# Expert products of 16 more tokens of block 2 from gathered U rows, in a decoder block on one Trainium2 core

## The chip, the cores and the metric

One core of one Trainium2 chip runs the kernel as one program. The metric is device time in microseconds (us) of one execution, the median of several runs. TensorE multiplies matrices, VectorE and ScalarE work on elements, GpSimd (POOL) does a few element operations here and writes the descriptors of indirect DMAs, SyncE (SP) issues most loads. All five run their own queues in order and meet through semaphores.

## The reference, cut to what matters

One layer of a decoder: a mixer (state-space heads beside latent attention) with a normalisation, and then PEER, an expert layer, with another. The change touches PEER alone:

```python
def peer(x, w_query, sub_keys, u_table, v_table):      # T = 128 tokens a block, 4 blocks
    ...
    def block(xb):
        q = (xb @ w_query).reshape(T, 8, 2, 128)
        s = jnp.einsum('thkd,hknd->thkn', q, sub_keys)
        sv, si = lax.top_k(s, 16)
        ...                                            # 16 of 16384 experts for each of 8 heads
        gate = jax.nn.softmax(top_s, axis=-1)
        u = jnp.take(u_table, expert_idx, axis=0)
        act = gelu(jnp.einsum('td,thkd->thk', xb, u))
        v = jnp.take(v_table, expert_idx, axis=0)
        return jnp.einsum('thk,thkd->td', gate * act, v)
```

Each of the 512 tokens has 128 experts; the tables hold 16384 rows of 1024 numbers each.

## The kernel before

Tokens are dealt with in two ways. **Dense:** U (16384 x 1024, loaded once as 128 chunks of 128 experts) is multiplied with all tokens of blocks 0 and 1 and the first half of block 2, so that a chunk's activations lie in `acts` as 128 experts x 320 tokens (`NU` = 320, `u_half`, L1402). Products are made of three float32r products each of rounded parts and remainders (`mm3`, L84): high part (`h`, ScalarE, L126) and low part (`l`, VectorE or GpSimd, L136) of each chunk of 128 x 1024. A chunk is 8 x 3 matmuls, done in two halves of 12. **Gathered:** for the other tokens the experts' rows themselves are fetched by indirect DMA, 128 rows of 4 KB at a time, one a partition, and VectorE multiplies each with its token's x and sums (a dot, L1140). In this way 64 tokens of block 2 (`UG` = 64) have their activations from 64 fetches; the halves of the partitions hold two experts of a token. Block 3 is done wholly by gathering, U rows and then V rows, behind.

V is multiplied densely for 384 tokens (`NT`): a matrix of gates (expert x token, mostly zeros) is built for them, G, multiplied with the activations and with V chunk by chunk (`v_chunk`, L1680; 18 matmuls of 512 columns). For the 64 gathered tokens the activations are multiplied into the gates already when these are made, so that their 64 columns of activations aren't read (L1638).

The order is emitted by hand: one Python program writes all queues. Around the change it is:

- `stage1` and `stage2` (L1031, L1113): top-16 searches and decoding of expert numbers, on VectorE. When block 2 is decoded, `ug_index` (L1119) writes the index list and issues the first four fetches (`UROWS` = 4 buffers `urow`).
- `build_g` (L1205): 48 groups `n` of 8 tokens. For each, VectorE makes `oj` (L1228) and `g` (L1234) one group ahead (`hot`), ScalarE scales half of `g` in the groups of `LOWA`, TensorE multiplies them (16 small matmuls, L1270 and L1271) into `pw`, ScalarE moves the result to `stg`, which is stored to DRAM. Each fourth group also multiplies finished gates into the activations at hand (L1294).
- In the same loop two dots of `ug_dots` (L1137) follow each group, and after every dot the fetch of the row four further (`ug_fetch`, L1131), into the buffer just read. When all are done, the activations of the second partition half go through DRAM to the first (L1144), and `ug_head` (L1150) multiplies them with the gates at groups 35 to 38.
- `drive` (L1465) puts U halves between: `tm[0]` sums the planned time of TensorE (3.6 a chunk, 1.2 a group), `tm[1]` that of VectorE (1.2 a dot, 1.2 a low part, and so on), and as long as the first isn't ahead, it emits another half, until chunk 76 (`AHEAD`), or 85 once `ug_dots` is done. In groups below 32 there are two stops for this: after `hot`, and after the dots. A half that begins a chunk also emits the high part of the chunk three further and the low part of the chunk two further (`Stream`, L93).
- Activations of chunks 0 to 49 stay in SBUF, those of 50 to 87 are spilled to DRAM (L1417).
- Behind it the V stage: U chunks from 85 on alternate with V chunks, beside them block 3's 256 dots (`gather`, L1525).

PSUM has eight banks: two `px`, four `pw`, two `pu` in this part.

## Time and profile before

| | |
|---|---|
| median of 3 runs | 1539.13 us (1536.28 to 1540.73) |
| the profiled execution | 1538.01 us; its span 1536.2 us |
| TensorE busy | 1519.5 us, 99% of the span |
| VectorE busy | 1353.5 us, 88% |
| ScalarE busy | 755.0 us, 49% |
| GpSimd busy | 646.0 us, 42% |
| TensorE's granted clock | 0.998 of full speed over the span |
| bytes moved by DMA | 418.58 MB |

Busy time counts an instruction from its start to its end, and matmuls overlap: one of 320 columns is busy 0.31 us but the next starts 0.147 us later. So TensorE's pace is read from starts. L with a number is a line of the kernel. In lists of groups, `out<-in` are the program's names, then come partitions x elements, the count, the busy time and the mean of one, and behind the bar the time for which the engine sat idle just before them, with what ended it. PE is TensorE, DVE VectorE, ACT ScalarE.

### The profile page before, as it was taken

The page shows a single profiled execution, that of the slowest core. Times are in us where ns is not written, and L with a number is a line of the kernel's source. Part 1 is how long each engine was busy: PE and PEld are TensorE (multiplying, and loading weights), DVE is VectorE, ACT ScalarE, POOL GpSimd, SP SyncE. Part 2 cuts the span into 40 slices and gives each one's busy share as a digit, 9 for nine tenths or more (in the row PEclk, how much of TensorE's full clock was granted, in tenths as well). Part 3 has the DMA queues.
Part 4 walks back from the last instruction along what each step waited for, and adds up shares of the span by engine and source line. Part 5 has one row for each costly group of instructions (what it writes and reads, how often), then busy time and mean ns, then how long its engine had stood idle before and what let it go on. Part 6 is the DMA issues. An engine that isn't in the chain of part 4 may idle for free.

```text
span 1536.2 us, 24606 instructions
## 1 busy us (share of the span) xinstructions
PE 1519.5 (99%) x8664; PEld 1338.5 (87%) x8664; DVE 1353.5 (88%) x2641; ACT 755.0 (49%) x1415; POOL 646.0 (42%) x472
## 2 busy tenths in 40 slices
PE   9999999999999999999999999999999999999997
PEld 7787888888888999999999988999999988888886
DVE  8979768746799999999999588999999999999997
ACT  5564477742433444666667544444444434444442
POOL 0000032420244522445430476666666667767610
PEclk9999999999999999999999999999999999999999
DMA  7243122475423566999998999999999999999983
GB/s 261 95 149 102 57 71 60 111 250 162 155 76 90 146 214 213 338 347 365 383 323 289 367 401 387 384 380 395 401 398 400 392 393 380 390 378 390 373 300 135
DMA packets 154028, 418.58 MB, mean 272 GB/s; under 512 B 15296, under 2 KB 57040, under 8 KB 153648
## 3 DMA queue, kind: packets, MB, share of 16 engines
q1 hardware_dynamic: 96000, 210.83, 39.7%
q0 software_dynamic: 52496, 187.74, 32.7%
q10 hardware_dynamic: 5408, 18.43, 3.0%
q8 instruction: 68, 1.11, 0.3%
q14 instruction: 56, 0.46, 0.1%
HBM read 384.08 MB, written 30.70 MB: 270 GB/s over the span
## 4 chain that ended last, share of the span: by engine, by line
PE 91%; DVE 5%; ACT 2%; DMA 1%; issue 1%; ACTq 0%; DVEq 0%
PE va L1675 11%; PE va L1674 11%; PE va L1678 11%; PE pu L85 10%; PE pu L87 10%; PE pu L86 10%; PE pw L85 3%; PE pw L86 3%; PE pw L87 3%; PE pa L86 3%; PE pa L87 3%; PE pa L85 3%; PE pw L1270 1%; PE pw L1271 1%; PE pb L534 1%; PE px L1008 1%
## 5 line engine op out<-in xcount | busy, mean ns | idle before, releaser
L126 ACT ACTIVATE wih<-wir 128x1024 fp32r<-128x1024 f32 (+2 forms) x269 | 277.0, 1031 | 128.8 <-PE va L1678 71.7
L136 DVE TENSOR_TENSOR wil<-wir,wih 128x1024 fp32r<-128x1024 f32 (+1 forms) x232 | 280.5, 1210 | 54.5 <-ACT wih L126 39.3
L87 PE MATMUL pu<-XT,wil 128*128 128x320 f32 x1000 | 309.3, 309 | 0.6 <-DVE wil L136 0.6
L1675 PE MATMUL va<-wil,Ph 128*128 128x512 f32 x726 | 283.1, 390 | 0.0
L1541 POOL DMA_INDIRECT row<-v,ix x128 | 217.6, 1700 | 99.6 <-DVE ac L1562 78.3
L1674 PE MATMUL va<-wih,Ph 128*128 128x512 f32 x606 | 236.2, 390 | 0.0
L1541 POOL DMA_INDIRECT row<-u,ix x128 | 180.2, 1408 | 131.9 <-DVE row L1556 69.5
L85 PE MATMUL pu<-XT,wih 128*128 128x320 f32 x664 | 208.4, 314 | 0.8 <-ACT aout L1416 0.8
L86 PE MATMUL pu<-XT,wih 128*128 128x320 f32 x664 | 205.2, 309 | 0.0
L87 PEld LDWEIGHTS pu<-XT,wil 128*128 128x128 f32 x1000 | 187.8, 188 | 0.9 <-DVE wil L136 0.9
L1678 PE MATMUL va<-wih,Pl 128*128 128x512 f32 x606 | 186.8, 389 | 0.0
L1562 DVE SCALAR_TENSOR_TENSOR ac<-row,hd,ac 128x1024 f32<-128x1024 f32 x128 | 164.2, 1283 | 4.6 <-DMA row<-v,ix 3.1
L1556 DVE SCALAR_TENSOR_TENSOR row<-row,XT 128x1024 f32<-128x1024 f32 x128 | 153.9, 1222 | 12.1 <-DMA row<-u,ix 11.4
L1675 PEld LDWEIGHTS va<-wil,Ph 128*128 128x128 f32 x726 | 136.4, 188 | 26.9
L1134 POOL DMA_INDIRECT urow<-u,uix x64 | 100.4, 1569 | 136.7 <-DVE urow L1140 120.8
L1657 ACT ACTIVATE Ph<-P 128x384 fp32r<-128x384 f32 x121 | 63.0, 520 | 155.9 <-DVE P L1634 141.1
L136 POOL TENSOR_TENSOR wil<-wir,wih 128x1024 fp32r<-128x1024 f32 (+3 forms) x37 | 77.8, 2110 | 145.1 <-ACT wih L126 120.9
L1678 PEld LDWEIGHTS va<-wih,Pl 128*128 128x128 f32 x606 | 113.7, 188 | 23.9
L1674 PEld LDWEIGHTS va<-wih,Ph 128*128 128x128 f32 x606 | 113.7, 188 | 22.7 <-ACT Ph L1657 0.3
L85 PEld LDWEIGHTS pu<-XT,wih 128*128 128x128 f32 x664 | 124.7, 188 | 2.3 <-ACT aout L1416 1.4
L86 PEld LDWEIGHTS pu<-XT,wih 128*128 128x128 f32 x664 | 124.8, 188 | 0.8
L85 PE MATMUL pu<-XT,wihx 128*128 128x320 f32 x336 | 104.9, 312 | 0.9 <-ACT aout L1416 0.9
(511 smaller groups left out, 3332.6 us busy)
## 6 DMA issues: line engine op xcount, KB each, us to landing
wir<-v SPq DMA_DIRECT2D x106, 512.0 KB, 7.1
wir<-ut SPq DMA_DIRECT2D x86, 512.0 KB, 6.1
wirx<-ut SPq DMA_DIRECT2D x42, 512.0 KB, 6.7
gt<-gsp SPq DMA_DIRECT2D x63, 256.0 KB, 9.2
wir<-wo SPq DMA_DIRECT2D x26, 512.0 KB, 4.2
wirx<-v SPq DMA_DIRECT2D x22, 512.0 KB, 7.0
gsp<-stg ACTq DMA_DIRECT2D x21, 448.0 KB, 6.4
wir<-wf SPq DMA_DIRECT2D x18, 512.0 KB, 3.3
```

Of the source, the lines that this page charges most:

```text
L85: T.matmul(ps, lh, rh, start=start, stop=False)
L86: T.matmul(ps, lh, rl, start=False, stop=False)
L87: T.matmul(ps, ll, rh, start=False, stop=stop)
L126: A.activation(h, r, AF.Copy)
L136: self.lo(n).tensor_tensor(l, r, h, op=OP.subtract)
L1134: G.indirect_dma_start(out=UR[n], out_offset=None, in_=I["u"], in_offset=bass.IndirectOffsetOnAxis(ap=UR["ix"][:, n:n + 1], axis=0))
L1541: G.indirect_dma_start(out=R[s], out_offset=None, in_=I["u"] if s < 128 else I["v"], in_offset=bass.IndirectOffsetOnAxis(ap=ix3[:, s % 128 ...
L1556: V.scalar_tensor_tensor(wide(r), wide(r), 1.0, x3, op0=OP.mult, op1=OP.mult, accum_out=hd[:, s:s + 1])
L1562: V.scalar_tensor_tensor(ac, r, hd[:, s - 128:s - 127], ac, op0=OP.mult, op1=OP.add)
L1674: T.matmul(va[b][e], Ph[b], h[:, cs], start=c == 0, stop=False)
L1675: T.matmul(va[b][e], Ph[b], l[:, cs], start=False, stop=False)
L1678: T.matmul(va[b][e], Pl[b], h[:, cs], start=False, stop=c == 127)
```

## The change

Sixteen more tokens of block 2 (tokens 48 to 63 of it) are gathered: `UG` = 80 fetches and dots. Dense U products are 304 columns wide (`NX`), while the activations keep 320 columns (`NU`), the last 16 set to one by a ScalarE copy.

- The 16 added fetches hold eight experts of a token each, in partition groups of 16 (`UB`). Their indices go through DRAM (`ixd`) into `uixb`, their x is loaded eight times over (`UR["xb"]`, in the free part of XT), and their results go through DRAM (`hbd`): one store and one load, both in ScalarE's queue, behind the last dot. The older results of 64 dots are moved as before, but already after dot 67.
- For the first 64 dots x lies in PSUM: `px`'s two banks are given up (`psG`, `xp`), two ScalarE copies fill them; uses of `px` take `pw` instead.
- A group with an even number is followed by three dots, an odd one by two. The head runs at groups 33 to 36 instead of 35 to 38.
- At the first stop of groups 0 to 24 (`BESIDE`) low parts of U chunks go to GpSimd, after a one-column memset of the output on VectorE, and don't count in `tm[1]`.
- A chunk is planned at 3.55 in place of 3.6; group 38 leaves `LOWA`; `digits` and `g_low` run together at group 10 of a block.

```diff
@@ -29,8 +29,11 @@
 NEG = -1.0e30
 SCALE = 192.0 ** -0.5
 NT = 384
-UG = 64
-NU = NT - UG
+UA = 64
+UB = 16
+UG = UA + UB
+NX = NT - UG
+NU = 320
 ND = NU // 32
 PIECES = 3
 FIRST = 44
@@ -44,14 +47,15 @@
 UROWS = 4
 RES = 3
 LASTC = 120
-T_U = 3.6
+T_U = 3.55
 T_Q = 6.3
 ROWS = 5
 GP = 4
 ENDU = 11
 WV = 0.86
+BESIDE = 25
 GST = (1, 3, 5, 7)
-LOWA = (*range(2, 32, 2), 34, 38)
+LOWA = (*range(2, 32, 2), 34)
 SCB = 6
 GSC = 2.0 ** 14
 BIG = 1.5 * 2.0 ** 26
@@ -133,7 +137,11 @@
                 self.his(n + 1 + self.ha)
                 r, h = self.raw.pop(n), self.hi.pop(n)
                 l = self.tiles(n, 1)[:, :r.shape[-1]]
-                self.lo(n).tensor_tensor(l, r, h, op=OP.subtract)
+                if beside[0]:
+                    V.memset(l[:, 0:1].bitcast(F32), 0.0)
+                    G.tensor_tensor(l, r, h, op=OP.subtract)
+                else:
+                    self.lo(n).tensor_tensor(l, r, h, op=OP.subtract)
                 self.w[n] = (h, l)
                 self.ns += 1
                 if self.xr and n % 4 == 3:
@@ -234,6 +242,8 @@
     xsp = dram.tile([NB, 128, D], F32, name="xsp")
     gsp = dram.tile([NT // 32, 128, 128, 32], F32, name="gsp")
     acd = dram.tile([64, 128], F32, name="acd")
+    ixd = dram.tile([UB, 128], I32, name="ixd")
+    hbd = dram.tile([128, UB], F32, name="hbd")
     asp = dram.tile([PRE - KEEP, 128, NU], F32, name="asp")
 
     wst = pool("wst")
@@ -261,6 +271,7 @@
     items = []
     plan = items.extend
     lo_on = [V]
+    beside = [False]
 
     wo_ = [I["wo"][k] for k in range(16)]
     ut_ = [I["ut"][i] for i in range(128)]
@@ -933,8 +944,8 @@
     close(psT)
     close(cs2)
 
+    psW = pool("psW", bufs=4, space=PSUM)
     psX = pool("psX", bufs=2, space=PSUM)
-    psW = pool("psW", bufs=4, space=PSUM)
     px = lambda: psX.tile([128, 512], F32, name="px")
     pw = lambda: psW.tile([128, 512], F32, name="pw")
 
@@ -944,9 +955,11 @@
     spare = lambda c0: XT[:, :, c0:c0 + 64].bitcast(F32)
     wide = lambda z: z.rearrange("p (a b) -> p a b", b=64)
     scl = xt.tile([128, 1], F32, name="scl")
+    one = xt.tile([128, NU - NX], F32, name="one")
+    V.memset(one, 1.0)
     ix3 = xt.tile([128, 128], I32, name="ix3")
     g3 = xt.tile([128, 128], F32, name="g3")
-    G0 = xt.tile([128, UG // 32, 8, 32], F32, name="G0")
+    G0 = xt.tile([128, NT // 32 - ND, 8, 32], F32, name="G0")
     xt.tile([128, 80], F32, name="edge")
     lnq = pool("lnq", side="right")
     ROW = lnq.tile([128, 2, D], F32, name="ROW")
@@ -1121,9 +1134,11 @@
         f = lambda z: z.rearrange("p h k -> p (h k)")
         ix = tmp[:, :128].bitcast(I32)
         V.scalar_tensor_tensor(ix, f(ijg[:, 0]), 128.0, f(ijg[:, 1]), op0=OP.mult, op1=OP.add)
-        G.dma_start(UR["ix"][:UG], ix[UG:, :UG])
-        V.tensor_copy(UR["ix"][UG:], ix[UG:, UG:])
-        G.dma_start(UR["g"], f(ijg[UG:, 2]))
+        G.dma_start(UR["ix"][:UA], ix[UA:, :UA])
+        V.tensor_copy(UR["ix"][UA:], ix[UA:, UA:])
+        G.dma_start(ixd, ix[UA - UB:UA])
+        G.dma_start(UR["g"][:UA], f(ijg[UA:, 2]))
+        G.dma_start(UR["g"][UA:], f(ijg[UA - UB:UA, 2]))
         for n in range(UROWS):
             ug_fetch(n)
         UR["dots"] = ug_dots()
@@ -1131,18 +1146,34 @@
     def ug_fetch(n):
         if n < UG:
             UR[n] = ug.tile([128, D], F32, name="urow", bufs=UROWS)
+            ap = UR["ix"][:, n:n + 1] if n < UA else UR["ixb"][:, n - UA:n - UA + 1]
             G.indirect_dma_start(out=UR[n], out_offset=None, in_=I["u"],
-                                 in_offset=bass.IndirectOffsetOnAxis(ap=UR["ix"][:, n:n + 1], axis=0))
+                                 in_offset=bass.IndirectOffsetOnAxis(ap=ap, axis=0))
 
     def ug_dots():
+        hd, hb = UR["hd"], UR["hdb"]
+        for e in range(2):
+            A.activation(wide(UR["xp"][:, e * 512:(e + 1) * 512]), UR["x"][:, e * 8:(e + 1) * 8], AF.Copy)
         for n in range(UG):
             r = UR.pop(n)
-            V.scalar_tensor_tensor(wide(r), wide(r), 1.0, UR["x"], op0=OP.mult, op1=OP.mult, accum_out=UR["hd"][:, n:n + 1])
+            if n < UA:
+                V.scalar_tensor_tensor(r, r, 1.0, UR["xp"], op0=OP.mult, op1=OP.mult, accum_out=hd[:, n:n + 1])
+            else:
+                V.scalar_tensor_tensor(wide(r), wide(r), 1.0, UR["xb"], op0=OP.mult, op1=OP.mult,
+                                       accum_out=hb[:, n - UA:n - UA + 1])
             ug_fetch(n + UROWS)
+            if n == 1:
+                G.dma_start(UR["ixb"], bass.AP(tensor=ixd.tensor, offset=ixd.offset, ap=[[UB, 128 // UB], [128, UB], [1, UB]]))
+            if n == UA + 3:
+                w = UR["w"]
+                A.activation(hd[UA:], hd[UA:], AF.Gelu)
+                nc.scalar.dma_start(w[:UA, UA:], hd[UA:])
+                A.activation(w[:UA, :UA], hd[:UA], AF.Gelu)
             yield 1.2
-        A.activation(UR["hd"][UG:], UR["hd"][UG:], AF.Gelu)
-        nc.scalar.dma_start(UR["w"][:, UG:], UR["hd"][UG:])
-        A.activation(UR["w"][:, :UG], UR["hd"][:UG], AF.Gelu)
+        A.activation(hb, hb, AF.Gelu)
+        nc.scalar.dma_start(hbd, hb)
+        nc.scalar.dma_start(UR["w"][UA:].rearrange("t (q n) -> t q n", n=UB),
+                            bass.AP(tensor=hbd.tensor, offset=hbd.offset, ap=[[UB, UB], [UB * UB, 128 // UB], [1, UB]]))
         close(ug)
         more_act(pool("act2"))
         yield 0.1
@@ -1158,20 +1189,24 @@
         V.reciprocal(r, mx)
         yield 0.7
         V.tensor_scalar(w, w, r, None, op0=OP.mult)
-        G.dma_start(scl[128 - UG:], mx)
+        G.dma_start(scl[UA:], mx[:UA])
+        G.dma_start(scl[UA - UB:UA], mx[UA:])
         yield 0.3
-        ps = px()
+        ps = pw()
         T.transpose(ps[:, :UG], w, ident[:UG, :UG])
-        gT = GT[2][1][:, 64 - UG // 2:]
-        gv = ps[:, :UG].rearrange("p (k c) -> p k c", c=2)
-        A.activation(gT[:, :, 0], gv, AF.Copy, scale=GSC)
+        gT = GT[2][1]
+        gs_ = [(gT[:, k0:k0 + n // 2], ps[:, c0:c0 + n].rearrange("p (k c) -> p k c", c=2))
+               for k0, c0, n in ((UA // 2, 0, UA), ((UA - UB) // 2, UA, UB))]
+        for g_, gv in gs_:
+            A.activation(g_[:, :, 0], gv, AF.Copy, scale=GSC)
         yield 0.1
-        V.scalar_tensor_tensor(gT[:, :, 1], gv, GSC, gT[:, :, 0], op0=OP.mult, op1=OP.subtract)
-        yield 0.2
+        for g_, gv in gs_:
+            V.scalar_tensor_tensor(g_[:, :, 1], gv, GSC, g_[:, :, 0], op0=OP.mult, op1=OP.subtract)
+        yield 0.3
 
     def g_head(b):
         ijg = IJG.pop(b)
-        ps = px()
+        ps = pw()
         for x, e in enumerate((1, 2, 0)):
             T.transpose(ps[:, x * 128:(x + 1) * 128], ijg[:, e].rearrange("p h k -> p (h k)"), ident)
         jT = ijp.tile([128, 64, 2], F16, name="jT", bufs=2)
@@ -1296,20 +1331,19 @@
             if b < 2:
                 if g == 9:
                     g_head(b + 1)
-                if g == 11:
+                if g == 10:
                     digits()
                     lump += 0.9
-                if g == 12:
                     g_low()
                     lump += 1.1
             lump += (1.45 if n + 1 in LOWA else 1.95) if n < 47 else 0.1
             if n < 32:
-                keep, least[0] = least[0], 0
+                keep, least[0], beside[0] = least[0], 0, n < BESIDE
                 yield lump
-                least[0], lump = keep, 0.0
-            for _ in range(2):
+                least[0], lump, beside[0] = keep, 0.0, False
+            for _ in range(3 - n % 2):
                 lump += next(dots, 0.0)
-            for _ in range({35: 2, 36: 1, 37: 1, 38: 1}.get(n, 0)):
+            for _ in range({33: 2, 34: 1, 35: 1, 36: 1}.get(n, 0)):
                 lump += next(head)
             yield lump
 
@@ -1401,19 +1435,21 @@
 
     def u_half(c, e, psum=None):
         if e == 0:
-            UO[c] = [z.rearrange("p (k j) -> p k j", k=8) for z in item()] + [(psum or pu)()[:, :NU]]
+            UO[c] = [z.rearrange("p (k j) -> p k j", k=8) for z in item()] + [(psum or pu)()[:, :NX]]
         h, l, ps = UO[c]
         for k in range(4 * e, 4 * e + 4):
-            mm3(ps, h[:, k], l[:, k], XTH[:, k, :NU], XTL[:, k, :NU], k == 0, k == 7)
+            mm3(ps, h[:, k], l[:, k], XTH[:, k, :NX], XTL[:, k, :NX], k == 0, k == 7)
         if e:
             del UO[c]
             t = None if away else act_tile()
             if t is not None:
                 ACT[c] = t
-                A.activation(t, ps, AF.Gelu)
+                A.activation(t[:, :NX], ps, AF.Gelu)
+                A.activation(t[:, NX:], one, AF.Copy)
             else:
                 t = out_.tile([128, NU], F32, name="aout", bufs=2)
-                A.activation(t, ps, AF.Gelu)
+                A.activation(t[:, :NX], ps, AF.Gelu)
+                A.activation(t[:, NX:], one, AF.Copy)
                 nc.sync.dma_start(asp[c - KEEP], t)
                 away.append(c)
 
@@ -1457,7 +1493,7 @@
         u_half(un[0], e)
         un[0] += e
         tm[0] += T_U / 2
-        if not e and lo_on[0] is V:
+        if not e and lo_on[0] is V and not beside[0]:
             tm[1] += 1.2
 
     un = [uc]
@@ -1495,17 +1531,24 @@
     drive(fill)
     close(rq)
     ug = pool("ug")
-    UR["x"], UR["x3"] = spare(448), spare(384)
-    for i in range(128 // UG):
-        G.dma_start(UR["x"][i * UG:(i + 1) * UG], wide(xsp[2, 128 - UG:]))
+    UR["x"], UR["x3"], UR["xb"] = spare(448), spare(384), spare(320)
+    for i in range(2):
+        G.dma_start(UR["x"][i * UA:(i + 1) * UA], wide(xsp[2, UA:]))
     G.dma_start(UR["x3"], wide(xsp[3]))
-    UR["ix"] = ijp.tile([128, UG], I32, name="uix")
-    UR["hd"] = ijp.tile([128, UG], F32, name="uhd")
+    for i in range(128 // UB):
+        G.dma_start(UR["xb"][i * UB:(i + 1) * UB], wide(xsp[2, UA - UB:UA]))
+    UR["ix"] = ijp.tile([128, UA], I32, name="uix")
+    UR["ixb"] = ijp.tile([128, UB], I32, name="uixb")
+    UR["hd"] = ijp.tile([128, UA], F32, name="uhd")
+    UR["hdb"] = ijp.tile([128, UB], F32, name="uhdb")
     UR["g"] = ijp.tile([UG, 128], F32, name="ugw")
     rt2 = pool("rt2")
     iaE = rt2.tile([128, 16, 16], F16, name="iaE")
     nc.sync.dma_start(iaE.rearrange("p a b -> p (a b)"), I["ch"][:, 256:512])
     lo_on[0] = V
+    close(psX)
+    psG = pool("psG", space=PSUM)
+    UR["xp"] = psG.tile([128, D], F32, name="xp")
     drive(stage2())
     close(rt2)
     close(rt)
@@ -1613,8 +1656,8 @@
     refill()
     if UO:
         step_u()
+    close(psG)
     close(psW)
-    close(psX)
 
     psV = pool("psV", space=PSUM)
     va = [[psV.tile([128, 512], F32, name=f"va{b}{e}") for e in range(2)] for b in range(3)]
```

## Rows read from the trace of the kernel before

**Rows 1.** The page, part 1: busy us (share of the span) and instructions.
```profile
PE 1519.5 (99%) x8664; PEld 1338.5 (87%) x8664; DVE 1353.5 (88%) x2641; ACT 755.0 (49%) x1415; POOL 646.0 (42%) x472
```
**Rows 2.** Busy time by stretch: us, busy of each engine, clock, DMA share, GB/s.
```profile
513.00:590.00 77.00, 77.00 (x530) 77.00 (x529) 76.11 (x189) 37.25 (x58) 23.35 (x15) 1.00 0.65 193
590.00:695.00 105.00, 104.35 (x861) 102.45 (x860) 99.05 (x137) 65.35 (x138) 44.99 (x30) 1.00 0.88 311
695.00:804.00 109.00, 107.23 (x883) 104.44 (x882) 104.47 (x144) 70.29 (x152) 46.55 (x32) 1.00 0.98 362
804.00:851.00 47.00, 46.66 (x436) 44.79 (x435) 42.88 (x52) 33.41 (x66) 6.17 (x12) 1.00 0.86 299
940.00:1240.00 300.00, 300.00 (x1653) 271.23 (x1652) 280.14 (x390) 126.32 (x220) 194.41 (x139) 1.00 1.02 394
```
**Rows 3.** Timeline of TensorE, matmuls 256 and 320 wide: start us, us.
```profile
208.34 0.28 PE L85 MATMUL pu<-wih,kvh 128*128 128x256 f32 x1
208.46 0.29 PE L86 MATMUL pu<-wil,kvh 128*128 128x256 f32 x1
...
511.04 0.31 PE L86 MATMUL pu<-XT,wihx 128*128 128x320 f32 x1
511.19 0.31 PE L87 MATMUL pu<-XT,wil 128*128 128x320 f32 x1
```
**Rows 4.** Groups of VectorE instructions from 590 to 804 us, shapes apart.
```profile
L1140 DVE SCALAR_TENSOR_TENSOR urow<-urow,XT 128x1024 f32<-128x1024 f32 x63 | 74.7, 1221 | 1.2 <-DMA urow<-u,uix 1.2
L136 DVE TENSOR_TENSOR wil<-wir,wih 128x1024 fp32r<-128x1024 f32 x39 | 47.6, 1221 | 5.9 <-ACT wih L126 3.7 <-issue 2.2
```
**Rows 5.** Timeline of VectorE: the two dots of one group.
```profile
661.61 1.22 DVE L1140 SCALAR_TENSOR_TENSOR urow<-urow,XT 128x1024 f32<-128x1024 f32 x1
...
662.76 1.22 DVE L1140 SCALAR_TENSOR_TENSOR urow<-urow,XT 128x1024 f32<-128x1024 f32 x1
```
**Rows 6.** Timeline of POOL: the fetches behind them; eight plain DMA issues.
```profile
663.11 1.68 POOL L1134 DMA_INDIRECT urow<-u,uix  x1 [2.34 <-DVE urow L1140]
665.09 1.44 POOL L1134 DMA_INDIRECT urow<-u,uix  x1 [0.30 <-DMA urow<-u,uix]
...
803.11 4.37 POOL L1397 DMA_DIRECT2D act<-asp  x8 [13.04 <-DVE urow L1140]
```
**Rows 7.** Landing of the fetches of `urow`, 590 to 695 and 695 to 804 us.
```profile
DMA to landing us min/median/max: 5.0/7.2/11.5
...
DMA to landing us min/median/max: 5.4/8.1/9.9
```
**Rows 8.** Timelines of POOL and VectorE, 398 to 403 us.
```profile
398.13 4.78 POOL L136 TENSOR_TENSOR wil<-wir,wih 128x1024 fp32r<-128x1024 f32 x2 [81.17 <-ACT wih L126]
...
397.80 1.28 DVE L966 SCALAR_TENSOR_TENSOR xm<-hres,pu 128x512 f32<-128x512 f32 x2
...
401.12 1.81 DVE L194 SCALAR_TENSOR_TENSOR lma<-lmy,lmh 128x1 f32<-128x1 f32 x1
...
403.16 0.22 DVE L194 SCALAR_TENSOR_TENSOR lma<-lmy,lmh 128x1 f32<-128x1 f32 x1
```
**Rows 9.** Last dot, gelu behind it, its store (KB, us to landing), head's start.
```profile
801.60 1.20 DVE L1140 SCALAR_TENSOR_TENSOR urow<-urow,XT 128x1024 f32<-128x1024 f32 x1
...
802.85 0.25 ACT L1143 ACTIVATE uhd<-uhd 64x64 f32<-64x64 f32 x1 [1.29 <-DVE urow L1140]
...
uw<-uhd ACTq DMA_DIRECT2D x1, 16.0 KB, 5.6
...
812.97 0.27 DVE L1153 TENSOR_TENSOR uw<-uw,ugw 64x128 f32<-64x128 f32 x1
```
**Rows 10.** The chain that ended last, one step in two chunk pairs.
```profile
960.60 0.46 PE va L1678 x2
...
968.22 0.46 PE va L1678 x2
```

## The prediction

> **What bounds the kernel now.** I read the page first: TensorE is busy 99% of the span and VectorE 88%, so a stage can have two engines at their limit at once [rows 1]. The table of busy time by stretch tells which is which [rows 2]. From 513 to 804 us both are full: VectorE works 76.1 of 77, 99.1 of 105 and 104.5 of 109 us. That is routing (513 to 590) and the gate matrices with the 64 gathered dots (590 to 804). From 804 to 851 TensorE is full and VectorE has 4 us free. From 940 to 1240 one U chunk and one V chunk alternate; TensorE is full, VectorE has 20 of 300 us free, and transfers run at 394 GB/s, the most of these stretches. In the chain of waits there the same step recurs after 7.62 us [rows 10]. The 24 products of the U chunk take 0.147 us each [rows 3], 3.53 us; that leaves 4.09 for the 18 of the V chunk, 0.227 each, as the chain shows them (0.46 for two). So TensorE sets that pace.
>
> A narrower product pays where TensorE alone is the limit, from 804 us on. Where VectorE is at its limit, the question is what the added dots do to it.
>
> **The narrower products.** Matmul starts are 0.147 us apart at 320 columns and 0.120 at 256 [rows 3], 0.42 ns a column; at 304 that gives 0.140. The saving is 6.7 ns for each of 128 x 24 = 3072 matmuls, 20.5 us if all of it counted, 0.16 a chunk. Chunks 0 to 2 run before 513 (0.5 us), 22 in 513 to 590 (3.5), some 50 up to 804, some 10 up to 851, and 43 behind (6.9). The weight load of each product still fits under 256 columns, so 304 lies inside what the rows show.
>
> **513 to 590.** VectorE has 0.9 us free there, so TensorE's 3.5 can give back 0.9 at most; I take 0.5. New here: eleven small loads in POOL's queue (x for the 16 tokens, indices, gates), 0.55 us of issue each [rows 6], and two ScalarE copies of x into PSUM. POOL is busy 23 of 77 us and ScalarE 37 [rows 2]; I cost them at nothing. Ahead of the first fetches stand two of the eleven, 1.1 us if nothing covered them.
>
> **590 to 804, the work of VectorE.** Busy now: 99.1 + 104.5 = 203.5 of 214 us. Added: 16 dots, 1.15 us from start to start [rows 5], 18.4. PSUM as second input: the 512-wide form that reads PSUM takes two in 1.28 us, like one dot of 1024 [rows 4, 8]; I take no difference, bounds 0 and 0.07 us a dot. Moved: with the planner's own sums followed through the loop (chunk 3.55, group 1.2, dot 1.2, low part 1.2), 13 low parts fall into the first stop of groups 0 to 24 and go to GpSimd, and chunk 77 in place of 76 is reached at group 33. A low part is busy 1.22 us [rows 4], 1.14 from start to start if it overlaps the next as the dots do: minus 14.8, plus 1.1 for the extra chunk, plus 13 memsets of one column, 0.2 each by the one-element instruction of rows 8, 2.6. Together 210.8, 7.3 more. TensorE's work shrinks by 8 us meanwhile, so VectorE alone is the limit, and the 10.5 us that it now idles would go.
>
> **590 to 804, the gathered rows.** This decides. There are four row buffers, so a row's fetch is issued when the dot four before it is done. POOL starts it 0.3 us after that dot's end and the next one 2.0 us later [rows 5, 6]. From issue to landing takes 7.2 us in the median before 695 and 8.1 after, from 5.0 to 11.5 [rows 7]. Now two dots of a group stand together, so four dots are two whole groups, nearly 13 us, and VectorE waited 1.2 us in all [rows 4].
>
> After the change groups take 3 and 2 dots in turn. The fifth dot of such a pair waits for the fetch that the first one frees, and between them lie two dots, the rest of one group and one dot. That rest is now (203.5 - 63 x 1.15) / 34 = 3.9 us, and 3.5 with the low parts moved. Lead: 2.3 + 3.5 + 1.15 = 6.95 us. Needed: 0.3 + 7.65 (the middle of the two medians) = 7.95. VectorE waits 1.0 us. Where a low part is ahead on POOL (2.4 us [rows 8], from the memset just before the first dot) the fetch can start 2.8 us after the burst of dots begins, in place of 1.45: VectorE waits 2.35. The first dot of a two-dot group hands its buffer to the third of the next burst with the same lead, lengthened by that wait, so it is late by 1.35 only where a low part stands in the odd group alone. With low parts in half of the groups up to 24 that is (1.0 + 3 x 2.35) / 4 = 2.0 us a pair, 12.5 pairs, 25 us; then 3.5 pairs at 1.0 to 1.5, 5 us. I take 30, because the medians are the nearest rows. Bounds: nothing with landings at the shortest of rows 7, 50 with landings at 9. VectorE then needs 241 us in place of 214: plus 27 (minus 3 to plus 47).
>
> **804 to 851.** TensorE has about one chunk less and the others are 0.16 us shorter: minus 4.8 of 47. Against that, the last 16 tokens' values go to DRAM and back, two hops in ScalarE's queue, the second waiting for the first. One such store of 16 KB took 5.6 us, and today the head's first multiply stands 10.2 us after the last dot's end, over 4 more than it needs [rows 9]. Two hops need some 12 us; the head is moved two groups earlier, about 6 us behind the last dot. So VectorE is held about 6 us there with the next groups' matrices behind it, and ScalarE 5.6 us at the second hop; behind that stand the evictions of the gate products, the rounded copies of U and the scaling for group 34, for which TensorE waits. I take plus 4.8, 0 in all (bounds -5 and +6).
>
> **From 851.** 43 chunks x 0.16 = 6.9 us. The 16 columns set to one are one more ScalarE copy a chunk, about 0.25 us (the shortest in rows 9), beside 126 busy of 300 us: nothing. The pair becomes 7.46 us, so the same bytes ask 394 x 7.62 / 7.46 = 402 GB/s, more than any stretch of rows 2 shows. I take 5 (bounds 0 and 6.9).
>
> **Sum.** The profiled execution took 1538.0 us, a span of 1536.2 and 1.8 around it. -0.5 - 0.5 + 27 + 0 - 5 = +21 gives 1559; the median of the runs lies 1.1 above the profiled one: 1560.
>
> **GpSimd beside VectorE.** While a low part ran on GpSimd, a VectorE instruction of one element with both inputs in SBUF took 1.81 us and ended with the low part; the same alone took 0.22. A 512-wide one with an input in PSUM went through as usual [rows 8]. The Trainium skill has it as a rule in "SBUF — State Buffer", section "Who interferes with whom": a VectorE instruction with two SBUF inputs and a GpSimd instruction that reads SBUF contend, and the second to issue blocks until the first is done. The trace agrees. By it the 64 dots from PSUM are safe, and `oj`, `g` and the low parts left on VectorE are not: rival 2.
>
> **Rivals** (times with the 1.1 added).
> 1. The rows land in time. It decides at a landing of 6.65 us (6.95 less 0.3) where no low part is ahead, at 5.3 where one is. For it: rows 7 reach down to 5.0, and a first wait spreads the burst. Against it: both medians. Then VectorE needs 211 of 214, the head costs 1 us less than TensorE saves, and nearly all of the last term comes: -0.5 - 0.5 - 3 - 1 - 6 = -11, 1528. Faster.
> 2. Low parts start late on POOL and hold VectorE. Dots cover 2.3 us in odd groups, less than the 2.4 of a low part, and 3.45 in even ones; POOL's third fetch ends some 6.9 us after the burst begins, just as the next memset comes. From any later end on, each of the 13 takes up to 2.4 us of `oj` or `g`. At 1.5 it is 20 us, half of it in place of waits for rows: 1570.
> 3. Rows land in time, but the two hops cost their 8 us beyond what TensorE saves: -0.5 - 0.5 - 3 + 8 - 5 = -1, 1538, no difference.
> 4. The products don't get shorter, because the weight loads set the pace: the savings go, 1567. The 0.120 at 256 columns speaks against it.
>
> **Chances.** Forecast 0.55, rival 1 0.22, rival 2 0.10, rival 3 0.10, rival 4 0.03. A measurement of this kernel tells about 0.3%, 4.6 us, from no change. Faster 0.23 (rival 1 and a little of 3), within 0.10, slower 0.67. The range takes in rival 1 and the long end of the landings, 1526 to 1578; the likeliest case alone has 1546 to 1578.
>
> **What would show it.** Matmul starts 0.140 apart in U chunks; dots waiting for their rows' DMA about 30 us, mostly the fifth of each pair; TensorE idle as much between 590 and 830; the last dot some 27 us later than now; the head's first multiply held near 6 us; a pair of chunks in 7.46 us. The prediction is wrong if the dots' waits stay under 10 us, or if the pair keeps 7.62.

## The result and the profile after

The changed kernel takes 1558.6 us in the median (1556.3 to 1563.3), the kernel before 1538.9 beside it on the same chip: a ratio of 1.0133, 95% interval 1.0105 to 1.0161. It is slower, by 19.7 us in the medians or 1.3%. The profiled execution after has a span of 1554.5 us; the 1536.2 of before makes 18.3 us between the two traces, and the points below split these 18.3.

First the stretches, as in [rows 2], with the columns of that group.

```profile
513.00:590.00 77.00, 76.68 (x552) 75.99 (x551) 75.92 (x188) 41.36 (x83) 27.70 (x25) 1.00 0.70 199
590.00:695.00 105.00, 99.10 (x809) 94.59 (x809) 93.41 (x141) 63.59 (x155) 55.55 (x41) 0.98 0.89 319
695.00:804.00 109.00, 101.54 (x819) 94.91 (x818) 96.75 (x145) 67.78 (x163) 61.92 (x46) 1.00 0.99 370
804.00:827.00 23.00, 16.40 (x134) 15.56 (x134) 22.29 (x30) 10.19 (x26) 5.98 (x6) 0.89 0.90 342
960.00:1240.00 280.00, 278.94 (x1572) 250.85 (x1571) 262.02 (x367) 124.14 (x246) 181.55 (x131) 1.00 1.02 396
```

Before the change TensorE was all but full from 590 to 804 (0.7 and 1.8 us free in the two stretches of [rows 2]); now it has 5.9, 7.5 and 6.6 us free in the three stretches up to 827, and VectorE has 11.6 and 12.3 us free in the first two, where it had 6 and 4.5. No compute engine is at its limit there any more: something is waited for. What it is stands in the groups of VectorE and GpSimd from the second dot to the last (599.6 to 824.3 us), which answer to [rows 4]:

```profile
L1160 DVE SCALAR_TENSOR_TENSOR urow<-urow,xp 128x1024 f32<-128x1024 f32 x63 | 75.6, 1218 | 19.0 <-DMA urow<-u,uix 18.4
L144 DVE TENSOR_TENSOR wil<-wir,wih 128x1024 fp32r<-128x1024 f32 x26 | 31.4, 1220 | 1.7 <-issue 1.7
L1162 DVE SCALAR_TENSOR_TENSOR urow<-urow,XT 128x1024 f32<-128x1024 f32 x16 | 19.1, 1221 | 2.7 <-DMA urow<-u,uixb 2.7
L142 POOL TENSOR_TENSOR wil<-wir,wih 128x1024 fp32r<-128x1024 f32 x10 | 23.9, 2394 | 37.3 <-DVE wil L141 25.8 <-ACT g L1273 5.9 <-ACT acts L1448 1.2
L142 POOL TENSOR_TENSOR wil<-wirx,wihx 128x1024 fp32r<-128x1024 f32 x3 | 7.2, 2403 | 4.3 <-ACT acts L1447 2.7 <-ACT wihx L130 0.8 <-ACT act L1448 0.8
```

A dot costs the same from PSUM (1218 ns) and from SBUF (1221). Thirteen low parts run on GpSimd at 2.4 us. The dots waited 21.1 us for the DMA of their rows, 1.2 before. The longest of these waits, in the timelines of VectorE and of POOL (start us, us, ..., in brackets the wait ahead of it):

```profile
648.84 1.22 DVE L1160 SCALAR_TENSOR_TENSOR urow<-urow,xp 128x1024 f32<-128x1024 f32 x1
...
654.45 1.22 DVE L1160 SCALAR_TENSOR_TENSOR urow<-urow,xp 128x1024 f32<-128x1024 f32 x1 [0.18 <-DMA urow<-u,uix]
...
659.96 1.22 DVE L1160 SCALAR_TENSOR_TENSOR urow<-urow,xp 128x1024 f32<-128x1024 f32 x1 [4.28 <-DMA urow<-u,uix]
```

```profile
649.07 2.37 POOL L142 TENSOR_TENSOR wil<-wir,wih 128x1024 fp32r<-128x1024 f32 x1 [1.15 <-issue]
651.59 1.21 POOL L1150 DMA_INDIRECT urow<-u,uix  x1 [0.15 <-issue]
```

The dot at 648.84 frees the buffer at 650.1. POOL is in a low part until 651.4, starts the fetch at 651.6, and the row is there 8.4 us later, at 659.96, when the fourth dot after it has been due since 655.7. So 1.5 us pass before the fetch starts, 1.2 more than the 0.3 us of [rows 5, 6], because of the low part ahead on POOL. The rest of the wait is that four buffers give a lead of 5.6 us here (650.1 to 655.7) for a landing of 8.4.

How the span divides, by the same landmarks in both traces (second dot, last dot, last gate product, first and last V product):

| | before | after | difference | forecast |
|---|---|---|---|---|
| up to the second dot | 599.8 | 599.6 | -0.2 | -1 |
| the dots' stage | 201.8 | 224.7 | +22.9 | +27 |
| last dot to last gate product | 51.4 | 49.9 | -1.5 | 0 |
| first to last V product | 663.8 | 661.7 | -2.1 | -5 |

The rest, two short pieces around the V products, is 0.8 us shorter. Two traces of the same code differ by 1.1 us in the dots' stage: e10 below leaves that stage as it was before and has 202.9, e9 leaves it as it is after and has 223.6. So 1 us in that row says little.

### The profile page after: what moved, and what is told of

Read it like the earlier page. It is cut to its first block, busy times and chain, and to the rows that moved or that the text cites. A ratio compares the mean times of both kernels' runs of the same rounds, so it can differ in the third digit from the quotient of the medians.

```text
span 1554.5 us, 24841 instructions
## 1 busy us (share of the span) xinstructions
PE 1514.0 (97%) x8664; PEld 1320.8 (85%) x8664; DVE 1360.3 (88%) x2672; ACT 765.9 (49%) x1539; POOL 685.5 (44%) x513
## 5 line engine op out<-in xcount | busy, mean ns | idle before, releaser
L91 PE MATMUL pu<-XT,wil 128*128 128x304 f32 x1000 | 302.8, 303 | 4.1 <-DVE wil L144 4.1
L144 DVE TENSOR_TENSOR wil<-wir,wih 128x1024 fp32r<-128x1024 f32 (+1 forms) x222 | 267.8, 1209 | 43.9 <-ACT wih L130 35.7
L1584 POOL DMA_INDIRECT row<-v,ix x128 | 222.4, 1737 | 94.8 <-DVE ac L1605 72.1
L89 PE MATMUL pu<-XT,wih 128*128 128x304 f32 x664 | 204.5, 308 | 3.1 <-ACT aout L1451 2.4
L90 PE MATMUL pu<-XT,wih 128*128 128x304 f32 x664 | 201.2, 303 | 0.0
L1718 PEld LDWEIGHTS va<-wil,Ph 128*128 128x128 f32 x726 | 136.2, 188 | 29.4 <-DVE wil L144 2.3
L1150 POOL DMA_INDIRECT urow<-u,uix x64 | 75.8, 1184 | 64.0 <-DVE urow L1160 53.6
L89 PE MATMUL pu<-XT,wihx 128*128 128x304 f32 x336 | 102.5, 305 | 0.6 <-ACT aout L1451 0.2
```

The source lines that it names most:

```text
L89: T.matmul(ps, lh, rh, start=start, stop=False)
L90: T.matmul(ps, lh, rl, start=False, stop=False)
L91: T.matmul(ps, ll, rh, start=False, stop=stop)
L144: self.lo(n).tensor_tensor(l, r, h, op=OP.subtract)
L1150: G.indirect_dma_start(out=UR[n], out_offset=None, in_=I["u"], in_offset=bass.IndirectOffsetOnAxis(ap=ap, axis=0))
L1584: G.indirect_dma_start(out=R[s], out_offset=None, in_=I["u"] if s < 128 else I["v"], in_offset=bass.IndirectOffsetOnAxis(ap=ix3[:, s % 128 ...
```

## The experiments

For all runs of whose stage of dots something is told, VectorE's account of that stage, from its busy time and from the waits ahead of the dots that a row's DMA ended; the rest is idle time for other reasons:

| kernel | stage | VectorE's work | waits for rows | other idle | first to last V product |
|---|---|---|---|---|---|
| before | 201.8 | 192.7 | 1.2 | 7.9 | 663.8 |
| after | 224.7 | 200.2 | 21.1 | 3.4 | 661.7 |
| e1, five row buffers | 211.0 | 199.2 | 8.6 | 3.2 | 663.6 |
| e2, six row buffers | 210.7 | 199.9 | 0.7 | 10.1 | 664.6 |
| e3, dots spread | 230.4 | 185.3 | 26.8 | 18.3 | 663.2 |
| e4, no low parts on GpSimd | 226.1 | 211.5 | 7.0 | 7.6 | 664.6 |
| e5, before with 304 columns | 200.9 | 193.1 | 1.0 | 6.8 | 664.0 |
| e6, after with 320 columns | 223.6 | 199.5 | 20.6 | 3.5 | 666.2 |
| e7, five rows, three stores | 204.5 | 199.0 | 4.3 | 1.2 | 664.4 |
| e8, before, three stores | 200.9 | 192.8 | 2.0 | 6.1 | 665.9 |
| e11, e5 with three stores | 200.7 | 193.2 | 3.6 | 3.9 | 662.1 |
| e12, e7, more on GpSimd | 211.8 | 204.7 | 6.3 | 0.8 | 664.8 |

### More row buffers (e1, e2)

The diff is that of e1; e2 has 6, 44 and 18.

```diff
-KEEP = 50
-MORE = 12
+KEEP = 47
+MORE = 15
...
-UROWS = 4
+UROWS = 5
```

> The changed kernel with five buffers for the gathered rows in place of four; three chunks of activations more are spilled to make room. Theory (the fetch of a row waits for the dot four before it, and a landing of 8 us is longer than the lead): a fifth buffer adds one dot and more to the lead, 2 to 4 us; the waits of dots for their rows fall from 21 us to 3 to 8 and the time from 1558 to 1543 (1538 to 1548). Rival bandwidth (the queues are full, more fetches in flight only land later): landing grows from 8.0 us to about 10, the waits stay above 15 us, the time stays within 3 of 1558. Rival low parts on GpSimd: no change.

> The changed kernel with six row buffers; six chunks more are spilled. Theory of the lead: waits of dots under 3 us, 1540 (1535 to 1545): hardly less than with five, since VectorE's own work of 211 us is then the limit. Rival bandwidth: landings of 12 us, waits as before, 1558. Either way the head's first multiply is held, as its two hops stay.

Five buffers: 1547.2 us, ratio 1.0052 (1.0036 to 1.0069), at the slow end of what I expected, with 8.6 us of waits where I had 3 to 8. Six: 1547.4, 1.0055 (1.0038 to 1.0072), which misses the 1535 to 1545. One more buffer takes 13.7 us off the stage, 12.5 of them waits for rows. That is the cause that the prediction named, and it is 11 of the change's 20 us in the medians. It speaks against rival bandwidth, whose waits stay; these two traces don't give the landings themselves. The sixth buffer ends the waits for rows as good as wholly, and gains nothing: VectorE then idles 10.1 us for other reasons. The room for the buffers comes from kept activation chunks, so more of them are spilled, and ScalarE stands longer before a store buffer is free (29.4 us in the stage of after). The list of waits from 600 to 831 us (engine, line, waited for: us, times, longest), of e1 and of e2:

```profile
ACT aout L1451 <- DMA asp<-aout: 35.6, 12, 4.9
```

```profile
ACT aout L1451 <- DMA asp<-aout: 42.5, 16, 5.5
...
DVE wil L144 <- issue: 4.9, 3, 3.8
DVE wil L144 <- ACT wih L130: 3.1, 2, 2.2
```

### The first dot of each group ahead of the matrices (e3)

```diff
-            lump = 0.0
+            lump = next(dots, 0.0) if n < 32 else 0.0
...
-            for _ in range(3 - n % 2):
+            for _ in range(2 - n % 2):
```

> The changed kernel with four buffers, but the first dot of each group put ahead of that group's two matrices, so that dots stand 1 and 2 (even groups) or 1 and 1 (odd) apart instead of 3 and 2 together. Theory of the lead: the shortest lead grows from 7 us to about 8.6 with no byte and no buffer more; waits fall from 21 to 6 us, 1544 (1539 to 1550). Rival bandwidth: waits stay, 1558. If only the count of buffers mattered and not the order, no change either.

A miss: 1577.6 us, 1.0247 (1.023 to 1.0264), slower than the change itself, with four buffers still. The waits for rows grew to 26.8 us, and two others came: VectorE's own low parts waited 8.2 us for ScalarE's high parts and 6.4 for GpSimd's low parts, and the part behind the last dot took 63.9 us. The run changes more than the order: the planner now emits more halves at the first stop, and 22 low parts go to GpSimd instead of 13. Its groups of POOL in the stage:

```profile
L142 POOL TENSOR_TENSOR wil<-wir,wih 128x1024 fp32r<-128x1024 f32 x15 | 35.9, 2393 | 10.1 <-issue 4.8 <-ACT g L1273 4.7 <-ACT wihx L130 0.5
...
L142 POOL TENSOR_TENSOR wil<-wirx,wihx 128x1024 fp32r<-128x1024 f32 x7 | 16.8, 2396 | 6.2 <-ACT wih L130 2.4 <-issue 2.4 <-ACT g L1273 1.4
```

Of 76 fetches 38 start more than 1.4 us behind the dot that frees their buffer, 28 in the changed kernel. So what spacing alone is worth isn't shown by this run; with nine more low parts ahead of the fetches it gains nothing.

### No low parts on GpSimd (e4)

```diff
-BESIDE = 25
+BESIDE = 0
```

> The changed kernel with all low parts of this stage back on VectorE (no group sends them to GpSimd). Theory: VectorE has 13 x 1.14 = 15 us more work less 13 memsets, but longer groups make the lead longer by 0.45 us and the fetches aren't held by low parts on POOL, so waits fall by about 9 us: 1562 (1557 to 1567). Rival 2 (low parts on GpSimd hold VectorE or the fetches by more than they save): faster, 1545 to 1552.

1562.2 us, 1.0156 (1.0128 to 1.0183). VectorE has 11.3 us more work, and the dots wait 14.1 us less: one fetch of 76 starts more than 1.4 us behind the dot that frees its buffer, in place of 28. With four buffers the low parts on GpSimd bring VectorE relief that the rows' lateness takes back. The stage is 1.4 us longer without them, little more than two traces of the same code differ by; and in this trace TensorE's granted clock was at 0.50 from 801 to 825 us.

### What the narrower products are worth alone, and what the rest costs without them (e5, e6)

The diff is that of e5 against the kernel before; e6 is the reverse on the changed kernel, `NX` back to `NU` in the products.

```diff
-            mm3(ps, h[:, k], l[:, k], XTH[:, k, :NU], XTL[:, k, :NU], k == 0, k == 7)
+            mm3(ps, h[:, k], l[:, k], XTH[:, k, :304], XTL[:, k, :304], k == 0, k == 7)
...
-                A.activation(t, ps, AF.Gelu)
+                A.activation(t[:, :304], ps, AF.Gelu)
+                A.activation(t[:, 304:], one, AF.Copy)
```

> The kernel before with one part of the change alone: the first-layer products of block 2 are 304 wide, and still only 64 tokens are gathered. Left out: the activations of 16 tokens, in whose place ScalarE copies ones (one short copy a chunk more, as in the changed kernel). So this is what the narrower products are worth when nothing has to be paid for them. Some 128 chunks of 24 products by 7 to 8 ns are 21 to 24 us of TensorE. My theory: the stage of the dots is bound by VectorE (10 us idle of 201.8) and gives back 0 to 2 us, the stage after the gate matmuls gives back 2 to 3 of its 6.9 because transfers run late there, the stages ahead 1: 1534 to 1537 us against 1539. Rival: TensorE's time counts everywhere, 1516 to 1520. Second rival: it counts in full after the gate matmuls and ahead of the dots, not beside them: 1531.

> The changed kernel with products 320 wide again; the 80 gathered tokens, their dots and everything else as changed (the 16 extra columns are computed and not used). So this is what the change costs without its saving. My theory: nothing is lost beside the dots (TensorE stands idle there for over 30 us, VectorE and the fetches set the time), 2 to 3 us after the gate matmuls and about 1 ahead of the dots: 1561 to 1564 us against 1558.6. Rival: the saving was there in full and the dots cost 41 instead of 20: 1578. Second rival: beside the dots TensorE's lateness adds up with the waits for the rows: 1567.

Narrow products alone: 1537.5 us beside 1539.5, 0.9997 (0.9986 to 1.0007): nothing, though 3072 products are 8 ns shorter each, 24.6 us of TensorE's time. That is next to the theory's 1534 to 1537 and far from both rivals. The stretches of e5 show where it stays:

```profile
600.00:800.00 200.00, 193.91 (x1652) 188.04 (x1651) 192.22 (x266) 135.76 (x329) 89.07 (x59) 1.00 0.95 347
...
960.00:1240.00 280.00, 277.13 (x1548) 247.96 (x1547) 263.20 (x364) 122.40 (x241) 184.96 (x129) 1.00 1.03 397
```

From 600 to 800 us TensorE now has 6.1 us free and VectorE is as full as before (192.2, 190.9 before); from 960 to 1240 TensorE has 2.9 us free, which it never had.

The changed kernel with wide products: 1566.0 us, 1.0174 (1.0157 to 1.0191), above my 1561 to 1564 and close to the second rival's 1567; but that rival's cause, lateness beside the dots, is not there. The dots' stage is the same (223.6 and 224.7), as expected. The V stage is 4.5 us longer than after, more than the 2 to 3 that I gave it, and 2.6 us stand ahead of the dots (second dot at 602.2; 599.8 before, 599.6 after, so there the saving pays for what the change adds). So the saving is worth 7.4 us in the changed kernel by the medians, 6 by the ratios, and none of it lies beside the dots. In the kernel before it is worth nothing as that stands, and with three store buffers 3.3 us by the medians, 4.5 by the ratios (e8 and e11, below).

### Three store buffers (e7, e8, e11)

```diff
-KEEP = 50
-MORE = 12
+KEEP = 48
+MORE = 14
...
-                t = out_.tile([128, NU], F32, name="aout", bufs=2)
+                t = out_.tile([128, NU], F32, name="aout", bufs=3)
```

This is e8, against the kernel before. e11 is the same on e5. e7 is the same on the changed kernel, with `UROWS` = 5, 46 kept and 16 more.

> The changed kernel with five row buffers (as in the run of five buffers, 1547.2 us, where VectorE was idle for 12.9 us of the 211.0 of the dots' stage), and now three buffers instead of two for the activations that ScalarE hands to the store into memory (ScalarE waited 35.6 us for them in that stage, in 12 places, longest 4.9). Room comes from 46 instead of 50 kept chunks. My theory: ScalarE held by the store delays the high parts, and VectorE's low parts behind them; with a third buffer ScalarE's waits for the store fall below 15 us, VectorE's idle time to 6 to 9 us, and the run to 1541 to 1544 us. Rival: the store only takes up time that ScalarE has over; VectorE's idle time stays at 11 to 13 us and the run at 1546 to 1549.

> The kernel before with the same edit: three store buffers instead of two, 48 instead of 50 kept chunks (14 instead of 12 fetched behind). There ScalarE waited 23.6 us for the stores in the stage of the dots, and VectorE was idle for 10.0 us of its 201.8. If ScalarE's waits for the store are the cause of VectorE's idle time: idle 5 to 7 us, 1534 to 1537 us. If not: 1538 to 1541.

> The kernel before with 304-wide first-layer products (the activations of 16 tokens left out, as in the narrow run, which gave 1537.5 us and 200.9 us for the dots' stage) and with three store buffers instead of two. Theory: beside the dots two things stand at the same limit in the kernel before, TensorE (200.0 us busy of 201.8) and ScalarE's waits for the stores with VectorE behind them; each edit alone gave back 0.9 us, and the two together give back 5 to 7: 195 to 197 us, run 1531 to 1533. Rival: VectorE's own work of 193 us and the rows set the stage: 200 to 201 us, run 1537 to 1538.

In the changed kernel with five rows the third store buffer is worth 6.7 us: 1540.4 beside 1539.5, 1.0007 (0.9997 to 1.0016). That is level with the kernel before. Its waits from 600 to 804 us and its stretch:

```profile
ACT aout L1451 <- DMA asp<-aout: 8.2, 10, 1.6
DVE urow L1160 <- DMA urow<-u,uix: 4.3, 4, 1.3
```

```profile
600.00:800.00 200.00, 197.51 (x1668) 191.25 (x1666) 194.50 (x292) 137.64 (x331) 119.75 (x88) 1.00 1.01 393
```

The waits for the store fell from 35.6 to 8.2 us. The stage lost 6.5 us: 4.3 of waits for rows, 2.0 of other idle time, 0.2 of work. I had put it down to late low parts alone; why the rows come earlier too isn't shown. What is left, 204.5 us, is 199.0 of VectorE's work, 4.3 of waits for rows and 1.2 of other idle time.

In the kernel before, the same buffer takes the waits for the store from 23.6 to 2.6 us, in the dots' stage before and in e8:

```profile
ACT aout L1416 <- DMA asp<-aout: 23.6, 10, 5.0
```

```profile
ACT aout L1416 <- DMA asp<-aout: 2.6, 2, 1.5
```

The time stays within 0.2% of where it was: 1537.1 beside 1539.5, 0.9987 (0.9975 to 0.9998). VectorE's idle time only falls from 9.1 to 8.1. With narrow products as well (e11) I expected 195 to 197 us for the stage; it is 200.7. So the theory that TensorE and the stores stood side by side at the limit of that stage falls. VectorE's 193 us and some 7 us in which it is idle make it up, 3.6 of them waits for rows; what sets the other 4 isn't shown. The run, 1533.8 beside 1540.9, 0.9958 (0.9942 to 0.9975), is between what the two theories gave; its trace has 1.1 us less in the stage, 1.1 behind it and 1.7 in the V stage than before.

### The V stage with half of block 3's rows (e9, e10)

```diff
-            if s < 256:
+            if s < 256 and s % 2 == 0:
                 R[s] = row(s)
...
-            r = R.pop(s)
+            r = R.pop(s) if s % 2 == 0 else r
```

> The changed kernel with every second row of block 3 left out of memory traffic: its 256 gathers of a row for each partition become 128, and two multiplications share one row (so block 3's values are others; VectorE's instructions are the same). This takes load from memory only in the stage behind the gate matmuls, which took 661.7 us, 663.8 before. Theory: that stage is now set by late weights, because memory delivers 396 GB/s whatever TensorE asks for; with fewer bytes it is set by TensorE alone, by the rows of both kernels 133.2 us of first-layer products and 2304 products of 0.227 us, 656 us; the run 1552 to 1554 us against 1558.6. Rival: the stage is held by TensorE's wait for something on the chip (low parts, activations): 661 to 662 us, run 1558 to 1559.

> The kernel before with the same edit, as a control: half of block 3's gathers left out. Theory: there TensorE sets the stage behind the gate matmuls (it is busy without a gap from 870 to 1520), so less traffic changes nothing: 663 to 664 us, run 1538 to 1540. Rival: memory held that stage before as well: 656 to 661 us, run 1532 to 1537.

With half of the gathers the V stage of the changed kernel takes 658.0 us in place of 661.7, near the 656 of TensorE alone, and the run 1554.1 us in place of 1558.6 (1.0091, 1.0075 to 1.0108). In the kernel before, the same edit does nothing: 664.5 us and 1539.4, 0.999 (0.998 to 1.0). TensorE's free 1.1 of 280 us in the last row of the stretches of after, above, and 1.2 of 270 in the row here are gone in e9. First the row of after, then the two of e9:

```profile
1250.00:1520.00 270.00, 268.82 (x1184) 221.70 (x1184) 260.93 (x320) 112.50 (x212) 174.15 (x100) 1.00 1.01 369
```

```profile
960.00:1240.00 280.00, 280.00 (x1581) 252.31 (x1581) 267.25 (x374) 125.25 (x249) 94.86 (x67) 1.00 0.86 281
1250.00:1520.00 270.00, 270.00 (x1192) 223.44 (x1192) 260.98 (x324) 113.09 (x215) 67.33 (x50) 1.00 0.87 272
```

And ScalarE's waits for the raw V weights from the first V product to the last, before and after; in e9 there is no such wait:

```profile
ACT wih L126 <- DMA wir<-v: 15.1, 9, 3.2
```

```profile
ACT wih L130 <- DMA wir<-v: 36.6, 18, 5.2
```

So it is the rate of transfers that keeps the shorter products from paying there. TensorE has no gap once the traffic falls to 281 GB/s, and has gaps at 396. The raw V weights come through SyncE's queue, so it is not GpSimd's issuing that held them up. Whether the memory or the 16 DMA engines (share 1.02 at 396) set that rate isn't shown.

### More low parts on GpSimd (e12)

Against e7:

```diff
-BESIDE = 25
+BESIDE = 32
```

> The changed kernel with five row buffers and three store buffers (1540.4 us, dots' stage 204.5 us with 199.0 us of VectorE), and low parts handed to GpSimd beside all of the stage's first 32 matrices of gate work instead of 25: some four more of them, 1.2 us of VectorE each. Theory: VectorE still sets that stage: 199 to 201 us, run 1535 to 1537, ahead of both kernels. Rival: memory sets it now (393 GB/s and all 16 engines busy from 600 to 800 us, as behind the gate matmuls): 204 to 205 us, run 1540 to 1541. Second rival: GpSimd is late with the fetches: above 1542.

A miss, and neither the theory nor the first rival: 1546.1 us, 1.0038 (1.0025 to 1.0052), the stage 211.8. The second rival has the time but not the cause: waits for rows grew by 2.0 of the stage's 7.3 us. Five more low parts went to GpSimd, and VectorE's work grew by 5.7 us. The groups of the stage, first of e7, then of e12:

```profile
L1263 DVE TENSOR_TENSOR oj<-iotaE,jT 128x1024 f16<-128x1024 f16 x31 | 22.3, 719 | 0.0
...
L1162 DVE SCALAR_TENSOR_TENSOR urow<-urow,XT 128x1024 f32<-128x1024 f32 x16 | 18.9, 1223 | 0.0
```

```profile
L1162 DVE SCALAR_TENSOR_TENSOR urow<-urow,XT 128x1024 f32<-128x1024 f32 x16 | 29.5, 1880 | 0.3 <-DMA urow<-u,uixb 0.3
...
L1263 DVE TENSOR_TENSOR oj<-iotaE,jT 128x1024 f16<-128x1024 f16 x31 | 24.1, 778 | 0.0
```

The last 16 dots, whose x lies in SBUF, take 10.6 us more together. The mean of 1.88 us hides how: eleven take 1.21 to 1.25 us as before, and five, each beside a low part on GpSimd, take 3.08 to 3.43 (shortest, median and longest in ns, behind the count):

```profile
L1162 DVE SCALAR_TENSOR_TENSOR urow<-urow,XT x16: 1211/1220/3426, 764.0 to 811.6; 128x1024 f32<-128x1024 f32 x16
```

One instance, GpSimd and then VectorE:

```profile
772.38 3.20 POOL L142 TENSOR_TENSOR wil<-wir,wih 128x1024 fp32r<-128x1024 f32 x1 [1.27 <-issue]
```

```profile
772.15 1.22 DVE L1162 SCALAR_TENSOR_TENSOR urow<-urow,XT 128x1024 f32<-128x1024 f32 x1
...
773.29 3.37 DVE L1162 SCALAR_TENSOR_TENSOR urow<-urow,XT 128x1024 f32<-128x1024 f32 x1
```

The low part takes 3.20 us instead of 2.4, as if it began at 773.2, about when the first dot ends (773.4); the second dot ends at 776.66, 1.1 us (one dot's pace) after the low part's end at 775.58. The durations fit the two running one after the other, whichever comes first. So in the changed kernel `BESIDE` = 25 and the 64 dots from PSUM belong together: group 25 is about where the dots from SBUF begin. This run therefore leaves open what it was made for, whether VectorE (199.0 of 204.5 us) or the transfers (393 GB/s, all 16 DMA engines busy) set e7's stage.

## Why the prediction was right, and where its steps were off

The sign, the place and the cause hold: the change loses its time in the dots' stage because the fetches of rows have too little lead, and TensorE's saving does not reach the end. 1558.6 was measured where 1560 was forecast, but that it came so near is in part luck. Between the two profiled executions it is +18.3 where the sum had +21, and errors cancel in it: +27 was 22.9 and -5 was -2.1; inside the 27 the waits were taken 10 us too long and the idle time that would go 6 us too long.

- **The products.** Starts are 0.139 us apart after (0.140 forecast from 0.147 and 0.120 in [rows 3]); rival 4 falls:

```profile
600.30 0.30 PE L89 MATMUL pu<-XT,wih 128*128 128x304 f32 x1
600.43 0.30 PE L90 MATMUL pu<-XT,wih 128*128 128x304 f32 x1
600.57 0.30 PE L91 MATMUL pu<-XT,wil 128*128 128x304 f32 x1
```

- **The work of VectorE.** Forecast +7.3, measured +7.5 (192.7 to 200.2). PSUM as a dot's input costs nothing, and 13 low parts moved, as the planner's sums gave. Their memsets took 0.8 us in all and not 2.6. e4 has the relief by itself, 11.3 us against the 12.2 of the working (14.8 less 2.6).
- **The waits for rows.** Forecast 30, measured 21.1, that is 19.9 more than before. The landing was about as taken from [rows 7] (8.0 in the median over the stage, as in the kernel before; 7.65 taken), so the step that failed is the lead, dot by dot. It was not mostly the fifth dot of a pair of groups: 10 of the 21 waits, with 13.9 us, are the third dot of the burst of three, which the first dot of the burst of two before it feeds, and only 4, with 3.9 us, the second dot of the burst of two, which the sum calls the fifth of the pair. The step saw that both have the same lead, and let the fifth dot's wait shield the third. It is the other way round: the third one's wait gives the fifth its time (from the end of the dot that frees the buffer to when the dot is due, 7.6 us in the mean for the thirds, 8.4 for the fifths), though 8 of the 13 low parts stand ahead of the fifth's fetch and 5 ahead of the third's (the instance above is one of these). e1 shows that this term is the cause; the instance above and e4 show that the low part ahead on POOL is in it, as the step said. TensorE was idle for 20 us between 590 and 827, where 30 were expected.
- **The idle time that would go.** 10.5 us were to be absorbed. Of 7.9 us other than waits for rows 4.5 went in the changed kernel, and only with a third store buffer does it come to 1.2 (e7) and 0.8 (e12). In e2 it is 10.1. The step took VectorE alone as the limit once TensorE's work shrinks; it left out that ScalarE waits for store buffers (23.6 us before, 29.4 after), and that its high parts are what VectorE's low parts need. With 19.9 + 7.5 - 4.5 = 22.9 the measured stage closes.
- **The bytes.** The working never asked what 16 fetches of 0.52 MB are to the transfers. The dots' stage moved 69.6 MB before and 80.2 MB after; the third row is e7 from 700 to 800 us, with 411 GB/s the highest that a trace here keeps for 100 us:

```profile
DMA packets 21579, 69.59 MB, mean 345 GB/s; under 512 B 2388, under 2 KB 5332, under 8 KB 21559
```

```profile
DMA packets 24943, 80.18 MB, mean 357 GB/s; under 512 B 2862, under 2 KB 6197, under 8 KB 24921
```

```profile
700.00:800.00 100.00, 97.69 (x819) 94.16 (x817) 96.56 (x142) 68.22 (x164) 54.52 (x39) 1.00 1.03 411
```

  As an estimate, 80.2 MB take 202.5 us at the 396 GB/s of the V stage and 195 at 411, where the stage took 201.8 before. So with every wait mended there is little or nothing to gain in it. Rival 1, in which the rows land in time, was priced at 1528, with 3 us less in this stage and 6 less in the V stage; e7, the run nearest to it, has 2.7 and 0.6 us more than before and comes to 1540.
- **From 804 us on.** Forecast 0, measured -1.5. The two hops were sized by the one store in [rows 9], 5.6 us. The first hop holds ScalarE 1.83 us, and the head's first multiply is held 1.5 us, not 6:

```profile
825.80 0.33 ACTq L1174 DMA_DIRECT2D hbd<-uhdb  x1
827.22 0.33 ACTq L1175 DMA_DIRECT2D uw<-hbd  x1
827.60 1.06 ACT L130 ACTIVATE wihx<-wirx 128x1024 fp32r<-128x1024 f32 x1 [1.83 <-DMA hbd<-uhdb]
```

```profile
832.62 0.29 DVE L1184 TENSOR_TENSOR uw<-uw,ugw 80x128 f32<-80x128 f32 x1 [1.49 <-DMA uw<-hbd]
```

  The store of 8 KB landed after 1.4 us, the load after 5.4; the head needs the matrices of group 34 and a multiplication into `acts` first (to 831.1), so most of the hops lie beside other work. Rival 3 falls. On the other side of the sum TensorE has one chunk less, as taken (208 U products for 232), but behind the last dot it waits 3.3 us for VectorE's gates (2.3 at 836.9, 1.0 at 873.3), where it was full before: about -4.8 + 3.3, not -4.8 + 4.8.
- **The V stage.** Forecast -5 with bounds 0 and 6.9, measured -2.1. The pair of chunks does keep 7.45 us where nothing is late, in 36 of the 39 pairs, and the U products saved 7.2 us (140.6 to 133.4, start to start). But V products came 2.7 us later beside them, 2.1 of it in three of the last five pairs (8.82, 7.57 and 8.05 us, all 7.45 in e9), and 2.4 us later behind them. Between kernels that differ in the width alone the stage gains 4.5 us (e6 to after), 3.8 (e8 to e11) and -0.2 (before to e5), 2.7 of the 7.2 in the mean. The text had the reason, 402 GB/s wanted and 394 the most seen, and took it for 1.9 us out of 6.9; e9 and e10 show that it was the decisive one. That was the row to go by.
- **Rival 2** did not happen: low parts beside PSUM dots ran at 2.4 us, and `oj` grew from 686 to 708 ns, 0.7 us in all. e12 shows such holds with dots from SBUF.

## What to carry to other kernels

Before work is moved from an engine to fetched operands, count the bytes of the stage against the highest rate that a trace holds over a stretch as long; where they come near the stage's present length, the change can gain little, however well the fetches are hidden. Give a gathered stream buffers by lead: the time between the work that frees a buffer and the work that needs it again must cover the landing plus whatever stands ahead of the fetch on the queue that issues it, at the tightest place of the rhythm and not on average. Time taken off an engine that is 99% busy was worth next to nothing here where another engine was busy for 95% of the same stage; a run with that saving alone tells this at once.
